# ScalarE takes 1-f and attention's output copies; x's sums keep their place; product orders change

## The chip, the cores and the metric

The program runs on one core of one Trainium2 chip. A time is device microseconds (us) of one execution. The kernel before has a median of 1113.62 us over three runs (1113.46 to 1114.1). Engines are named as the profile does: PE is TensorE, DVE is VectorE, ACT is ScalarE, POOL is GpSimd; SP starts DMAs. The profile is of one execution, and its lines are lines of the kernel before.

## The reference, cut to what matters

One layer over 256 tokens of width 2048, all in float32. The input is normed and projected to nine parts. Five of them belong to sixteen heads of a gated linear recurrence (q, v, forward gates, backward gates, output gate z_a), four to a short convolution, which the change leaves alone.

```python
hn = _rmsnorm(h, norm_w[i])
proj = hn @ w_in[i]
q, v, f_fwd, f_bwd, z_a, b_gate, c_gate, h_b, z_b = jnp.split(proj, IN_SPLITS, axis=-1)
# per direction:
f = lb + (1.0 - lb) * jax.nn.sigmoid(f_logit)
log_f = jnp.log(f)
k = 1.0 - f
# chunks of 64 tokens: q and k times exp of running sums of log_f, scores, masked, times v,
# plus what a carried state adds; forward and backward are summed
o_a = _head_rmsnorm(o_a, hgrn_norm_w[i]) * jax.nn.silu(z_a)
...
h = h + jnp.concatenate([o_a, o_b], axis=-1) @ w_out[i]
gate = jax.nn.sigmoid(h @ w_ple_gate[i])
h = h + (p[i] @ w_ple[i]) * gate
return _rmsnorm(h, final_norm_w)
```

So `k = 1 - f` is an affine map of the sigmoid, with two numbers per channel.

## The kernel before, in words

**Weights.** SP's queue loads tiles of w_in (128 x 2048 f32, `raw`, three buffers). The class `Stream` splits each half tile into a high and a low part, which together carry the value: ScalarE casts the high part (L121) and VectorE subtracts it to get the low one (L122). A split tile (`spl`, five buffers) is asked for three ahead of the products that read it. Splits are most of the work of both engines.

**Products.** A gate block (`gemm_in`) projects 256 channels: 16 k-tiles, each with four products on PE, two 128x512 ones (L428: high weights against both parts of x) and two 128x256 ones (L426: low weights against x's high part). A table `kicks` gives single k-tiles another order of these four: PLAIN is long, short, long, short; OUTER is long, short, short, long; SHORTS is both shorts and then both longs. `evac` sums the two halves of an accumulator (ScalarE copies one, L488, VectorE adds the other, L489).

**Stages.** Two heads are a pair. `two_pairs(i)` runs for i = 0, 2, 4, 6: for the pairs i and i+1 the blocks FF, FB (both gates) and Q, then `gemm_vz`, which makes v and z_a of four heads at once. For i = 2, 4, 6 three of its eight pairs of k-tiles are multiplied with seven products of sums in place of eight; for that, sums of x (`xsum`, from `xd`; `act_sums` L533 and L536, `act_split` L543 and L544) are made once, in the stage of i = 0, or whenever the scheduler lets them in.

**Attention's elementwise work.** `mix_forgets` of a pair: GpSimd multiplies by the tokens' norms (L493), ScalarE takes sigmoids (L615, L617), and for each direction and head the logarithm `lf` (L624, an ACTIVATE with a scale and a bias per channel); VectorE turns the sigmoid into 1-f in place (L628, the same kind of map, 128x256, four per pair). `mix_pair`: VectorE's scans of `lf` (L679, L685), differences (L692 to L703), ScalarE's exponentials (L704 to L707), VectorE's products with k and q (L708, L709), GpSimd's `kc`, `qc`, `kx` (L717, L723). PE's scores (L736) and `cx` (L780), then masks and copies. `outputs`: PE's four outputs `o` in PSUM (L798, L799), ScalarE's sums of squares of `o` (L803), VectorE's copy of `o` to `ogz` in SBUF (L804, 128x512, one per pair).

**The end of two pairs.** A stage later `finish_two` takes the square root of the mean squares (L643, ScalarE, 128x8), its reciprocal (L644) and scales `ogz` with it and with the output gate `zt` (eight 128x128 pieces, L649, VectorE). `turn` transposes each pair's `ogz` on PE (L659, four per pair) and splits it into `mixa` (L662, L663), from which the output projection reads.

**What sets the order.** A tile scheduler places each engine's instructions by priority; `tc.high_priority(offset=...)` lifts splits and sums of accumulators ahead of other work, and `tc.keep_in_program_order` pins an instruction to its written place. Attention's pieces are started at due times: `at(n, f)` calls f after n further ticks, and each k-tile of products ticks once. Within an engine the queue is then fixed; an instruction waits for its inputs, and all behind it wait too. Each time when ScalarE changes between functions of different tables, the program has an ACT_TABLE_LOAD.

Of the kernel before, what the change touches and what calls it, by code (L numbers as in the profile page):

```python
# [17 lines left out]
P = 128  # L18
# [119 lines left out]
def tile_hymba_encoder(  # L138
# [118 lines left out]
    cvw, th = vec[:, 3:6, :], vec[:, 6:10, :].rearrange("p (d j) c -> p d j c", d=2)  # L257


    wz = const.tile([P, P], F32, name="wz")  # L260
    dve.memset(wz, 0.0)

    act.activation(dummy[:, 0:1], wz[:, 0:1], AF.Copy)
# [8 lines left out]
    ones = const.tile([P, 1], F32, name="ones")  # L272
    pool.memset(ones, 1.0)

    early = const.tile([P, 2048], F32, name="early")
    smask = early[:, 0:T]
    pool.memset(smask, 1.0)
    pool.memset(smask.rearrange("p (c t) -> p c t", t=CH)[:, :, 0:1], 0.0)
# [16 lines left out]
        dve.memset(t, 0.0)  # L295


    mx = const.tile([P, 2, 16], F32, name="mx")
    et = const.tile([P, 2, 2, 16], F32, name="et")
    esum = const.tile([P, 2, 16], F32, name="esum")  # L300
# [72 lines left out]
    rbc = const.tile([P, T], F32, name="rbc")  # L373
    rbc2 = early[:, T : 2 * T]
    ss8 = const.tile([P, 2, 4], F32, name="ss8")
    rw = [const.tile([P, P], F32, name=f"rw{m}") for m in range(2)]

    def load_tokens(m):
        nc.sync.dma_start(xf32[:, 8 * m : 8 * m + 8].rearrange("p k t -> p (k t)"), xtok[:, m])
# [12 lines left out]
    def x_norms():  # L392
        dve.tensor_reduce(out=rx, in_=ss8, op=ALU.add, axis=AX.X)
        act.activation(rx, rx, AF.Sqrt, bias=epst, scale=1.0 / D)
        dve.reciprocal(out=rx, in_=rx)
        for m in range(2):
            dve.tensor_copy(rw[m], rx[:, m : m + 1].broadcast_to([P, P]))

    def norms_spread():
        rps = psm.tile([P, 512], F32, tag="y", name="rps")  # L400
        for m in range(2):
            pe.matmul(rps[:, m * P : (m + 1) * P], lhsT=rw[m], rhs=ident, start=True, stop=True)
        dve.tensor_copy(rbc, rps[:, :T])  # L403
        dve.tensor_tensor(out=rbc2, in0=rbc, in1=rbc, op=ALU.mult)

# [121 lines left out]
    at(14, norms_spread)  # L527


    def act_sums(src, a, s):  # L530


        dve.tensor_tensor(out=a, in0=src[:, :, 0], in1=src[:, :, 1], op=ALU.add)  # L533
        a11, a21, a12, a22 = (a[:, k, m * P : (m + 1) * P] for k in range(2) for m in range(2))
        for o, x, y in ((0, a21, a22), (1, a21, a11), (2, a11, s[:, 0]), (3, a12, s[:, 2])):
            dve.tensor_tensor(out=s[:, o], in0=x, in1=y, op=ALU.subtract)  # L536
# [74 lines left out]
    def mix_forgets(i, xf, qt):  # L611

        by_norms(xf.rearrange("p a b t -> p (a b) t"), rbc, 4)
        by_norms(qt, rbc, 2)
        act.activation(xf, xf, AF.Sigmoid)  # L615
        sg = ap_.tile([P, 2, T], F32, tag="sg", name=f"sq{i}")
        act.activation(sg, qt, AF.Sigmoid)  # L617
        pool.tensor_tensor(out=qt, in0=qt, in1=sg, op=ALU.mult)

        lf = ap_.tile([P, 2, 2, T], F32, tag="lf", name=f"lf{i}")  # L620
        for d in range(2):
            for h in range(2):
                hd = 2 * i + h
                act.activation(  # L624
                    lf[:, d, h, :], xf[:, d, h, :], AF.Ln,
                    bias=lb[:, d, hd : hd + 1], scale=oml[:, d, hd : hd + 1],
                )
                dve.tensor_scalar(  # L628
                    xf[:, d, h, :], xf[:, d, h, :], noml[:, d, hd : hd + 1], oml[:, d, hd : hd + 1],
                    op0=ALU.mult, op1=ALU.add,  # L630
                )
        return lf

# [34 lines left out]
    def mix_pair(i, xf, qt, lf, here=False):  # L668
# [121 lines left out]
        def outputs(vt, ogz, ss):  # L790

            s, sx = st
            o = psm.tile([P, 2, 2, P], F32, tag="y", name=f"o{i}")
            for h in range(2):
                c = (2 * (i % 2) + h) * P
                hs = slice(c, c + P)
                for m in range(2):
                    pe.matmul(o[:, m, h, :], lhsT=s[:, h, m, :], rhs=vt[:, m, hs], start=True, stop=False)  # L798
                    pe.matmul(o[:, m, h, :], lhsT=sx[:, h, 1 - m, :], rhs=vt[:, 1 - m, hs], start=False, stop=True)  # L799
            junk = ap_.tile([P, P], F32, tag="jk", name=f"jk{i}")  # L800
            for h in range(2):
                for m in range(2):
                    act.activation(junk, o[:, m, h, :], AF.Square, accum_out=ss[:, m, h : h + 1])  # L803
            dve.tensor_copy(ogz, o)  # L804

        return scores, outputs

# [5 lines left out]
    def two_pairs(i):  # L813
# [455 lines left out]
```

## Time and profile before

| | |
|---|---|
| median of 3 runs | 1113.62 us (1113.46 to 1114.1) |
| the profiled execution | 1113.2 us |
| its span in the trace | 1111.2 us |
| granted TensorE clock, mean | 0.998 |
| PE busy | 1100.2 us (99%), 6455 matmuls |
| VectorE busy | 854.4 us (77%) |
| ScalarE busy | 675.4 us (61%) |
| GpSimd busy | 267.1 us (24%) |
| L628, 1-f on VectorE | 32 x 442 ns = 13.9 us (with overlap) |
| L804, output copies on VectorE | 8 x 680 ns = 5.4 us |

Times in a timeline are microseconds from the span's start. The stages of two pairs begin, by PE's first product of each, at 7, 128, 240 and 357 us; the convolution's blocks begin at 475 us. An instruction's row in a timeline has its start, its duration, engine and line, and in brackets what ended the idle time ahead of it. A mean duration is longer than the time from start to start where an engine overlaps two instructions.

### The profile page before, as it was taken

The page shows a single profiled execution, that of the slowest core. Times are in us where ns is not written, and L with a number is a line of the kernel's source. Part 1 is how long each engine was busy: PE and PEld are TensorE (multiplying, and loading weights), DVE is VectorE, ACT ScalarE, POOL GpSimd, SP SyncE. Part 2 cuts the span into 40 slices and gives each one's busy share as a digit, 9 for nine tenths or more (in the row PEclk, how much of TensorE's full clock was granted, in tenths as well). Part 3 has the DMA queues.
Part 4 walks back from the last instruction along what each step waited for, and adds up shares of the span by engine and source line. Part 5 has one row for each costly group of instructions (what it writes and reads, how often), then busy time and mean ns, then how long its engine had stood idle before and what let it go on. Part 6 is the DMA issues. An engine that isn't in the chain of part 4 may idle for free.

```text
span 1111.2 us, 16886 instructions
## 1 busy us (share of the span) xinstructions
PE 1100.2 (99%) x6455; PEld 947.7 (85%) x6455; DVE 854.4 (77%) x1127; ACT 675.4 (61%) x946; POOL 267.1 (24%) x215
## 2 busy tenths in 40 slices
PE   9999999999999999999999999999999999999997
PEld 8888888888888888888888888888888888888886
DVE  7899468996889778998657848856767888877673
ACT  7787567767876697675535534534546575575562
POOL 1035116103430325043333223424331000000101
PEclk9999999999999999999999999999999999999999
DMA  9755555474447844658999998999979987887542
GB/s 349 271 166 172 183 190 169 135 265 152 159 147 263 305 152 152 224 171 234 299 305 262 255 340 222 289 328 264 290 202 297 326 297 286 288 312 251 196 133 76
DMA packets 69808, 260.44 MB, mean 234 GB/s; under 512 B 7008, under 2 KB 16608, under 8 KB 52192
## 3 DMA queue, kind: packets, MB, share of 16 engines
q1 hardware_dynamic: 60480, 242.25, 62.1%
q0 software_dynamic: 8960, 16.78, 9.8%
q8 instruction: 51, 0.84, 0.3%
q10 hardware_dynamic: 288, 0.34, 0.1%
q14 instruction: 29, 0.24, 0.1%
HBM read 257.25 MB, written 35.65 MB: 264 GB/s over the span
## 4 chain that ended last, share of the span: by engine, by line
PE 93%; DVE 3%; POOL 1%; issue 1%; ACT 1%; DMA 0%; DVEq 0%; ACTq 0%
PE a L428 36%; PE a L426 18%; PE avz L548 3%; PE avz L549 3%; PE avz L550 3%; PE pg L1030 3%; PE pg L1031 3%; PE pg L1029 3%; PE pa L548 2%; PE pa L550 2%; PE pa L549 2%; DVE spl L122 1%; PE pb_sc L550 1%; PE pb_sc L548 1%; PE pb_sc L549 1%; PE cx L780 1%
## 5 line engine op out<-in xcount | busy, mean ns | idle before, releaser
L122 DVE TENSOR_TENSOR spl<-raw,spl 128x1024 fp32r<-128x1024 f32 (+2 forms) x419 | 505.1, 1222 | 165.4 <-ACT spl L121 158.2
L428 PE MATMUL a<-xs,spl 128*128 128x512 f32 x1792 | 621.9, 393 | 0.6 <-DVE xs L368 0.6
L121 ACT CAST spl<-raw 128x1024 fp32r<-128x1024 f32 (+2 forms) x419 | 413.0, 999 | 250.3 <-PE a L426 96.4
L426 PE MATMUL a<-xs,spl 128*128 128x256 f32 x1792 | 494.8, 279 | 0.0
L428 PEld LDWEIGHTS a<-xs,spl 128*128 128x128 f32 x1792 | 334.0, 187 | 74.0 <-ACT spl L121 0.7
L426 PEld LDWEIGHTS a<-xs,spl 128*128 128x128 f32 x1792 | 337.1, 189 | 2.9 <-DVE spl L122 0.3
L1146 POOL TENSOR_TENSOR hh<-hh,fw 128x512 f32<-128x512 f32 (+1 forms) x9 | 10.9, 1225 | 250.7 <-ACT gt L1145 248.0
L488 ACT COPY r<-a 128x256 f32<-128x256 f32 x112 | 40.4, 368 | 34.6 <-PE a L426 33.0
L548 PE MATMUL avz<-spl,xs 128*128 128x512 f32 x138 | 54.0, 391 | 0.0
L550 PE MATMUL avz<-spl,xs 128*128 128x512 f32 x138 | 53.7, 389 | 0.0
L549 PE MATMUL avz<-spl,xs 128*128 128x512 f32 x138 | 53.7, 389 | 0.0
L717 POOL TENSOR_TENSOR qc<-pf,ge 128x256 f32<-128x256 f32 x16 | 22.0, 1379 | 106.7 <-ACT dd L707 89.1
L1029 PE MATMUL pg<-spl,ht 128*128 128x512 f32 (+1 forms) x120 | 45.2, 377 | 0.0
L1030 PE MATMUL pg<-spl,ht 128*128 128x512 f32 (+1 forms) x120 | 45.0, 375 | 0.0
L1031 PE MATMUL pg<-spl,ht 128*128 128x512 f32 (+1 forms) x120 | 45.0, 375 | 0.0
L493 POOL TENSOR_TENSOR xf<-xf,rbc 128x1024 f32<-128x1024 f32 x8 | 20.8, 2603 | 96.9 <-DVE rbc L403 49.5
L121 ACT CAST spl<-early 128x1024 fp32r<-128x1024 f32 (+1 forms) x29 | 28.7, 990 | 19.6 <-PE pb_y L550 7.5
L122 DVE TENSOR_TENSOR spl<-early,spl 128x1024 fp32r<-128x1024 f32 (+1 forms) x29 | 32.8, 1147 | 8.3 <-ACT spl L121 7.8
L548 PE MATMUL pa<-spl,mixa 128*128 128x512 f32 x88 | 34.5, 392 | 0.0
L550 PE MATMUL pa<-spl,mixa 128*128 128x512 f32 x88 | 34.3, 390 | 0.0
L549 PE MATMUL pa<-spl,mixa 128*128 128x512 f32 x88 | 34.3, 389 | 0.0
L946 POOL TENSOR_TENSOR cg<-cg,hb 128x512 f32<-128x512 f32 x8 | 13.7, 1718 | 79.2 <-DVE hb L489 79.2
(321 smaller groups left out, 1650.5 us busy)
## 6 DMA issues: line engine op xcount, KB each, us to landing
raw<-in_w_in_dram SPq DMA_DIRECT2D x106, 1024.0 KB, 7.0
raw<-in_w_in_dram SPq DMA_DIRECT2D x100, 256.0 KB, 3.9
raw<-in_w_out_dram SPq DMA_DIRECT2D x36, 512.0 KB, 5.6
sums<-in_w_out_dram SPq DMA_DIRECT2D x32, 512.0 KB, 10.4
raw<-in_w_in_dram SPq DMA_DIRECT2D x26, 512.0 KB, 5.5
raw<-sums SPq DMA_DIRECT2D x13, 1024.0 KB, 5.2
raw<-in_w_gate_dram SPq DMA_DIRECT2D x9, 1024.0 KB, 4.9
sums<-in_w_out_dram POOLq DMA_DIRECT2D x16, 512.0 KB, 10.5
```

The source lines that it names most:

```text
L121: self.nc.scalar.copy(out=v[:, :, 0], in_=r)
L122: self.nc.vector.tensor_tensor(out=v[:, :, 1], in0=r, in1=v[:, :, 0], op=ALU.subtract)
L426: pe.matmul(a[:, :T], lhsT=lhsT, rhs=xs[:, kt, 0, :], start=False, stop=(kt == NKT - 1))
L428: pe.matmul(a, lhsT=lhsT, rhs=xs[:, kt, :, :].rearrange("p s n -> p (s n)"), start=(kt == 0), stop=False)
L488: act.copy(out=r, in_=acc[m][:, 1, :])
L548: pe.matmul(acc, lhsT=ah, rhs=w[:, 0], start=start, stop=False)
L549: pe.matmul(acc, lhsT=ah, rhs=w[:, 1], start=False, stop=False)
L550: pe.matmul(acc, lhsT=al, rhs=w[:, 0], start=False, stop=stop)
L717: pool.tensor_tensor(out=c64(dst[:, d]), in0=c64(src[:, d, :, half * P : (half + 1) * P]), in1=g.unsqueeze(3).broadcast_to([P, 2, 2, CH]), ...
L1029: pe.matmul(acc[m], lhsT=lh, rhs=wh, start=(kt == 0), stop=False)
L1030: pe.matmul(acc[m], lhsT=lh, rhs=wl, start=False, stop=False)
L1031: pe.matmul(acc[m], lhsT=ll, rhs=wh, start=False, stop=(kt == nk - 1))
```

## The change

1. In `mix_forgets` 1-f moves from VectorE (`tensor_scalar`) to ScalarE (`activation` with Identity, the same scale and bias per channel): 32 instructions.
2. In `outputs` the copy of `o` moves from VectorE to ScalarE: 8 instructions.
3. The first instruction of each of x's sums keeps its place in program order.
4. Three k-tiles of pair 1's FB block (1, 5 and 9) go from one SHORTS (at 1) to three; the Q blocks of pairs 5 and 7 become plain (before: OUTER at 1, SHORTS at 5).
5. A few small tiles move to other buffers: `wz` into `early`, `mx`, `et` and `esum` into the pool `xp`, both `rw` into one tile with the tag of the scores.

```diff
@@ -257,7 +257,8 @@
-    wz = const.tile([P, P], F32, name="wz")
+    early = const.tile([P, 2048], F32, name="early")
+    wz = early[:, 1024 : 1024 + P]
     dve.memset(wz, 0.0)
...
-    mx = const.tile([P, 2, 16], F32, name="mx")
+    mx = xp.tile([P, 2, 16], F32, name="mx")
...
-    rw = [const.tile([P, P], F32, name=f"rw{m}") for m in range(2)]
...
+        rw.append(ap_.tile([P, 2, P], F32, tag="s", name="rw"))
...
-    def act_sums(src, a, s):
+    def act_sums(src, a, s, place=lambda instr: instr):
...
-        dve.tensor_tensor(out=a, in0=src[:, :, 0], in1=src[:, :, 1], op=ALU.add)
+        place(dve.tensor_tensor(out=a, in0=src[:, :, 0], in1=src[:, :, 1], op=ALU.add))
...
-                dve.tensor_scalar(
-                    xf[:, d, h, :], xf[:, d, h, :], noml[:, d, hd : hd + 1], oml[:, d, hd : hd + 1],
-                    op0=ALU.mult, op1=ALU.add,
+                act.activation(
+                    xf[:, d, h, :], xf[:, d, h, :], AF.Identity,
+                    bias=oml[:, d, hd : hd + 1], scale=noml[:, d, hd : hd + 1],
                 )
...
-            dve.tensor_copy(ogz, o)
+            act.copy(out=ogz, in_=o)
...
-                act_sums(xs[:, k : k + 2], a, t)
+                act_sums(xs[:, k : k + 2], a, t, tc.keep_in_program_order)
...
-            kicks = {(0, 1): ({}, ONE, BOTH), (2, 0): (ONE, BOTH, {}), (2, 1): ({}, {}, {})}
-            kicks |= {(4, 0): (ONE, TURNED, BOTH), (6, 0): (ONE, TURNED, BOTH)}
+            kicks = {(0, 1): ({}, {k: SHORTS for k in (1, 5, 9)}, BOTH), (2, 0): (ONE, BOTH, {}), (2, 1): ({}, {}, {})}
+            kicks |= {(i, e): ((ONE, TURNED, BOTH), ({}, {}, {}))[e] for i in (4, 6) for e in range(2)}
             kick = kicks.get((i, e), ({}, {}, BOTH if i + e else {}))
```

The scheduler moves more than the diff says. In the order of a program `spl` is a weight split, `ss` the squares' sums and their root, `ogz` the attention outputs, `pf`, `dd` and `ge` the exponentials' tiles, `sq` and `sz` the sigmoids of q and z_a, `r` the copy of an accumulator half, `x<-y` means that x is written from y; in the changed kernel lines from L400 on are numbered two higher.

ScalarE in the stage of i = 4, from pair 4's first exponentials on, the kernel before:

```order
L706 ACT_TABLE_LOAD
L706 ACTIVATE pf_2755<-dd_2756 128x512
L643 ACT_TABLE_LOAD
L643 ACTIVATE ss_1332<-ss_1332,epst 128x8
L121 CAST spl_2830<-raw_2809 128x4x256
L617 ACT_TABLE_LOAD
L617 ACTIVATE sq_2737<-qt_2354 128x512
L121 CAST spl_2851<-raw_2849 128x4x256
L638 ACTIVATE sz_0_2749<-zt_1331 128x512
```

The square root of pairs 2 and 3 stands behind the first exponential, ahead of the sigmoids. ScalarE with the change, where the square root stands now:

```order
L490 COPY r<-a_5_0_2786 128x256
L490 COPY r<-a_5_1_2787 128x256
L121 CAST spl_2926<-raw_2895 128x4x256
L709 ACT_TABLE_LOAD
L709 ACTIVATE dd_2754<-dd_2754 128x512
L121 CAST spl_2947<-raw_2945 128x4x256
L645 ACT_TABLE_LOAD
L645 ACTIVATE ss_1330<-ss_1330,epst 128x8
L121 CAST spl_2992<-raw_2945 128x4x256
```

It stands behind the sigmoids, behind the last of pair 4's exponentials and behind six more splits. The order for i = 6 changes in the same way.

VectorE in the same stage before, from the reciprocal of that root on:

```order
L644 RECIPROCAL ss_1332<-ss_1332 128x8
L122 TENSOR_TENSOR spl_2830<-raw_2809,spl_2830 128x4x256
L709 TENSOR_TENSOR pf_2755<-qt_2354,pf_2755 128x512
L122 TENSOR_TENSOR spl_2851<-raw_2849,spl_2851 128x4x256
L649 SCALAR_TENSOR_TENSOR ogz_2447<-ogz_2447,ss_1332,zt_1331 128x128 x2
L649 SCALAR_TENSOR_TENSOR ogz_2704<-ogz_2704,ss_1332,zt_1331 128x128 x2
L122 TENSOR_TENSOR spl_2878<-raw_2849,spl_2878 128x4x256
L649 SCALAR_TENSOR_TENSOR ogz_2447<-ogz_2447,ss_1332,zt_1331 128x128 x2
```

The scalings are spread among splits. VectorE with the change:

```order
L710 TENSOR_TENSOR dd_2754<-xf_2351,dd_2754 128x512
L122 TENSOR_TENSOR spl_2947<-raw_2945,spl_2947 128x4x256
L646 RECIPROCAL ss_1330<-ss_1330 128x8
L651 SCALAR_TENSOR_TENSOR ogz_2445<-ogz_2445,ss_1330,zt_1329 128x128 x4
L122 TENSOR_TENSOR spl_2992<-raw_2945,spl_2992 128x4x256
L651 SCALAR_TENSOR_TENSOR ogz_2702<-ogz_2702,ss_1330,zt_1329 128x128 x2
L491 TENSOR_TENSOR xf_2784<-a_5_0_2874,r 128x256
L651 SCALAR_TENSOR_TENSOR ogz_2702<-ogz_2702,ss_1330,zt_1329 128x128 x2
```

The reciprocal follows the root to its new place, and the scalings of the first pair stand together ahead of the second pair's. PE's transposes of `ogz` stand where they did.

x's sums on VectorE: before, two of the three start in the first pair's stage, behind the tokens' squares.

```order
L393 TENSOR_REDUCE few<-ss_176 128x2
L533 TENSOR_TENSOR xd<-xs 128x512
L536 TENSOR_TENSOR xd<-xd 128x128 x4
L533 TENSOR_TENSOR xd<-xs 128x512
L395 RECIPROCAL few<-few 128x2
L397 COPY rw_177<-few 128x128
```

With the change they stand in the stage of i = 2, between its splits.

```order
L122 TENSOR_TENSOR spl_1375<-raw_1354,spl_1375 128x4x256
L535 TENSOR_TENSOR xd<-xs 128x512
L538 TENSOR_TENSOR xd<-xd 128x128 x4
L122 TENSOR_TENSOR spl_1403<-raw_1401,spl_1403 128x4x256
L546 TENSOR_TENSOR xsum<-xd,xsum 128x4x128
```

More of the change, by code (lines that the diff above doesn't have):

```diff
@@ L273, in tile_hymba_encoder @@
     pool.memset(ones, 1.0)
-    early = const.tile([P, 2048], F32, name="early")
     smask = early[:, 0:T]
@@ L295, in tile_hymba_encoder @@
         dve.memset(t, 0.0)
-    mx = const.tile([P, 2, 16], F32, name="mx")
-    et = const.tile([P, 2, 2, 16], F32, name="et")
-    esum = const.tile([P, 2, 16], F32, name="esum")
+    mx = xp.tile([P, 2, 16], F32, name="mx")
+    et = xp.tile([P, 2, 2, 16], F32, name="et")
+    esum = xp.tile([P, 2, 16], F32, name="esum")
     lb = const.tile([P, 2, 16], F32, name="lb")
@@ L395, in x_norms @@
         dve.reciprocal(out=rx, in_=rx)
+        rw.append(ap_.tile([P, 2, P], F32, tag="s", name="rw"))
         for m in range(2):
-            dve.tensor_copy(rw[m], rx[:, m : m + 1].broadcast_to([P, P]))
+            dve.tensor_copy(rw[0][:, m], rx[:, m : m + 1].broadcast_to([P, P]))
+    rw = []
     def norms_spread():
@@ L401, in norms_spread @@
         for m in range(2):
-            pe.matmul(rps[:, m * P : (m + 1) * P], lhsT=rw[m], rhs=ident, start=True, stop=True)
+            pe.matmul(rps[:, m * P : (m + 1) * P], lhsT=rw[0][:, m], rhs=ident, start=True, stop=True)
         dve.tensor_copy(rbc, rps[:, :T])
```

## The prediction

> **What bounds the kernel now.** I read the page's head and its chain of waits first, then the timelines of the engines by stage. The head and the chain:
>
> ```profile
> span 1111.2 us, 16886 instructions
> PE 1100.2 (99%) x6455; PEld 947.7 (85%) x6455; DVE 854.4 (77%) x1127; ACT 675.4 (61%) x946; POOL 267.1 (24%) x215
> PE 93%; DVE 3%; POOL 1%; issue 1%; ACT 1%; DMA 0%; DVEq 0%; ACTq 0%
> ```
>
> TensorE is busy for 99% of the span and is 93% of the chain. So a lighter VectorE is worth nothing by itself: the change can only win where PE waits or paces slowly, and loses wherever it makes PE wait. Between its first product and the tail I find one real wait of PE. It stands in the first pair's stage, here in PE's timeline with the two engines behind it (start, duration, engine, line; idle before in brackets):
>
> ```profile
> 113.12 1.16 PE L780 MATMUL cx<-qc,kx 128*128 128x128 f32 x8 [1.06 <-POOL kx L723]
> ...
> 111.16 1.91 POOL L723 TENSOR_TENSOR kx<-kc,ge 128x512 f32<-128x512 f32 x1
> ...
> 99.98 0.63 ACT L706 ACTIVATE pf<-dd 128x512 f32<-128x512 f32 x1 [5.11 <-DVE gx L701]
> ```
>
> PE waits 1.06 us for GpSimd's kx, which hangs on the exponentials, for which ScalarE had idled 5.11 us behind VectorE.
>
> **1-f and the copies, unit prices.** In the groups by line (count, busy us, mean ns, idle before):
>
> ```profile
> L628 DVE TENSOR_SCALAR xf<-xf,noml,oml 128x256 f32<-128x256 f32 x32 | 13.9, 442 | 4.6 <-ACT lf L624 4.6
> L624 ACT ACTIVATE lf<-xf,lb,oml 128x256 f32<-128x256 f32 x32 | 18.3, 597 | 0.1
> L804 DVE COPY ogz<-o 128x512 f32<-128x512 f32 x8 | 5.4, 680 | 1.1 <-ACT jk L803 1.1
> L787 ACT COPY sx<-cx 128x512 f32<-128x512 f32 x8 | 4.6, 579 | 5.1 <-PE cx L780 5.1
> ```
>
> VectorE loses 13.9 + 5.4 us. The trace has no Identity; its nearest row is L624, of the same shape with the same two per-partition operands: 597 ns, and 0.50 us from start to start (two of them fill 274.24 to 275.23 below). A copy takes 0.50 us likewise (579 ns, overlapped). In total ScalarE gains 32 x 0.50 + 8 x 0.50 = 20 us, and at 61% busy it has room. What matters is where.
>
> **The turn of pairs 4 and 5 (and 6 and 7), the main term.** In the middle of a block PE turns the previous pairs' outputs, eight transposes of ogz, and then goes on with that block's products:
>
> ```profile
> 301.04 1.03 PE L659 MATMUL ogt<-ident,ogz 128*128 128x128 f32 x8
> 301.83 0.48 PE L428 MATMUL a<-xs,spl 128*128 128x512 f32 x1
> ...
> 418.54 1.03 PE L659 MATMUL ogt<-ident,ogz 128*128 128x128 f32 x8
> ```
>
> They stand at the same places of PE's order before and after; the first four read one ogz, the last four the other, from 301.04 + 4 x 0.11 = 301.47. Each ogz is first scaled on VectorE (L649), which needs the reciprocal (L644) of ScalarE's square root (L643). In ScalarE's timeline before:
>
> ```profile
> 269.48 1.06 ACT L615 ACTIVATE xf<-xf 128x1024 f32<-128x1024 f32 x1 [1.46 <-POOL xf L493]
> ...
> 274.24 1.09 ACT L624 ACTIVATE lf<-xf,lb,oml 128x256 f32<-128x256 f32 x2
> 275.23 1.03 ACT L121 CAST spl<-raw 128x1024 fp32r<-128x1024 f32 x1
> ...
> 277.65 0.28 ACT L803 ACTIVATE jk<-o 128x128 f32<-128x128 f32 x1 [0.88 <-PE o L799]
> ...
> 283.95 0.30 ACT L643 ACTIVATE ss<-ss,epst 128x8 f32<-128x8 f32 x1
> ...
> 288.55 0.63 ACT L638 ACTIVATE sz<-zt 128x512 f32<-128x512 f32 x1 [0.47 <-POOL qt L618]
> ...
> 299.87 1.03 ACT L121 CAST spl<-raw 128x1024 fp32r<-128x1024 f32 x1
> ```
>
> The square root ran at 283.95, 17 us ahead of the transposes. The order of the changed kernel puts it right ahead of the split that began at 299.87, behind both gates' sigmoids and the last exponential. From the sigmoid at 269.48 to that split the two orders hold the same ScalarE work, seven table loads each, but for four Identities and one output copy more. The sigmoid's start cannot move: it waits for GpSimd, which waits for PE's scores. So the split starts at 299.87 + 4 x 0.50 + 0.50 = 302.4, less the waits of ScalarE in that stretch (0.88 + 0.47 + 0.1 about an exponential), which a fuller queue swallows: its squares come at 278.2, after PE's output at 277.65. That is 300.9, and the square root ends at about 301.0. I see no new wait in the stretch: the chunk decays' inputs are ready by 279.9, ScalarE comes to them at 280.8.
>
> Behind it VectorE still has to work, by these rows:
>
> ```profile
> 284.76 0.19 DVE L644 RECIPROCAL ss<-ss 128x8 f32<-128x8 f32 x1
> ...
> 291.57 1.48 DVE L649 SCALAR_TENSOR_TENSOR ogz<-ogz,ss,zt 128x128 f32<-128x128 f32 x4 [1.20 <-POOL zt L639]
> 292.98 1.21 DVE L122 TENSOR_TENSOR spl<-raw,spl 128x1024 fp32r<-128x1024 f32 x1
> ...
> 297.07 0.75 DVE L489 TENSOR_TENSOR xf<-a,r 128x256 f32<-128x256 f32 x2
> 297.74 0.60 DVE L649 SCALAR_TENSOR_TENSOR ogz<-ogz,ss,zt 128x128 f32<-128x128 f32 x2
> ```
>
> In its new order: reciprocal 0.2, four scalings 1.4 (292.98 - 291.57), a split 1.1, two scalings 0.5, one sum of accumulators 0.3, two scalings 0.6: 4.1 us, with 0.1 for handing over. The second ogz is ready at 305.25, PE wants it at 301.47: **a wait of 3.8 us**, with everything on PE queued behind it, and nothing later that would give it back, since PE is the bound to the end. The stage of pairs 6 and 7 is a copy of this one 117.5 us later (418.54 against 301.04) with the same new order: 3.8 us again. **Sum +7.6 us.** Bounds: an Identity as cheap as the narrower copies L488 (two in 0.5 us, so 0.25) gives 2.8 a turn; ScalarE's waits all remaining gives 5.3. With Identities and copy free it would be 1.3. I take 3.8, since L624 is the same form.
>
> **The first pair.** VectorE's groups from 54 to 95.3 us, where it had nearly no idle time:
>
> ```profile
> L628 DVE TENSOR_SCALAR xf<-xf,noml,oml 128x256 f32<-128x256 f32 x8 | 4.3, 543 | 0.0
> L536 DVE TENSOR_TENSOR xd<-xd 128x128 f32<-128x128 f32 x8 | 3.0, 409 | 0.1
> L544 DVE TENSOR_TENSOR xsum<-xd,xsum 128x512 fp32r<-128x512 f32 x3 | 2.0, 681 | 0.0
> L533 DVE TENSOR_TENSOR xd<-xs 128x512 f32<-128x512 f32 x1 | 0.7, 692 | 0.0
> ```
>
> 10.0 us leave this stretch: 1-f to ScalarE, x's sums to the next stage (128 to 157 us), where VectorE waits at every split and both find room. ScalarE gets eight Identities (4.0 us), loses three casts of the sums (0.6 each) and its 5.11 us wait. The last logarithm stays near 90 us, VectorE is ready for the scans at about 91.5 instead of 95.4, so exponentials and kx come about 4 us earlier; 1.06 is all PE can gain. **-1.06 us** (0 if ScalarE slips by 3 us there).
>
> **Pairs 2 and 3.** Here PE runs close to its suppliers (VectorE's rows, then PE's):
>
> ```profile
> 200.01 0.42 DVE L489 TENSOR_TENSOR qt<-a,r 128x256 f32<-128x256 f32 x1
> ...
> 207.06 0.85 DVE L122 TENSOR_TENSOR spl<-raw,spl 128x512 fp32r<-128x512 f32 x1
> ...
> 203.79 0.62 ACT L121 CAST spl<-raw 128x512 fp32r<-128x512 f32 x1
> ...
> 211.01 0.39 PE L548 MATMUL ey<-spl,xsum 128*128 128x512 f32 x1
> ```
>
> Up to the 512-wide split ScalarE gets four Identities and one table load more (1.30 us from start to start), while a copy of 0.5 moves behind: 203.79 + 2.0 + 1.3 - 0.5 = 206.6, end 207.2, so VectorE starts its part 0.14 late, and the piece that PE reads at 211.01, done 0.1 us before, comes just in time. I take **0**, bounds 0 and +1.
>
> The Trainium skill, page "ScalarE: Activation LUTs", section "What ACT_TABLE_LOAD costs", counts 2.66 us for a switch, load and drain; by it this piece would be 1.4 us late and the sum 1.4 higher. The trace's 1.30 is used.
>
> **Product orders.** PE's timeline, fifteen k-tiles in the plain block and in the next one with two changed k-tiles:
>
> ```profile
> 289.94 0.39 PE L428 MATMUL a<-xs,spl 128*128 128x512 f32 x1
> ...
> 300.34 0.39 PE L428 MATMUL a<-xs,spl 128*128 128x512 f32 x1
> ...
> 302.61 0.39 PE L428 MATMUL a<-xs,spl 128*128 128x512 f32 x1
> ...
> 313.18 0.40 PE L548 MATMUL avz<-spl,xs 128*128 128x512 f32 x1
> ```
>
> 10.40 us plain, 10.57 with the changed order, which throws PE into the slower of its two steady paces (the first stages run in it too). Two such blocks turn plain: **-0.34 us**, or 0 if PE comes out of the wait in the slow pace. The block that gets three changed k-tiles runs in the slow pace; a changed k-tile there did not end it, so 0, at best -0.3 for that block and the next. The tiles that move into other buffers touch nothing but the first microseconds, where GpSimd's fill now follows the 13 warming products and GpSimd is idle until 53 us: 0.
>
> **Sum:** 7.6 - 1.06 - 0.34 = +6.2. The profiled execution took 1113.2 us (span 1111.2, 2.0 around it), the median of the runs is 1113.62: **1119.8 us**, a span of about 1117.4.
>
> **Rivals.** (1) *Half the price*: the added ScalarE work costs next to nothing in that stretch, so the turns wait 1.3 us each: 1113.62 + 2.6 - 1.4 = 1114.8. For it: ScalarE idles 39% of the time. Against it: from 269 to 301 it idles 1.5 us in all. (2) *Not slower*: ScalarE's queue runs ahead far enough that the square root still clears the transposes. Place: the split at 299.87; it decides if the square root ends before 297.2, 3.8 us ahead of my sum; then only the gains are left, 1112.2. For it: VectorE feeds the exponentials sooner. Against it: ScalarE waits for VectorE nowhere in that stretch, and L624 never takes under 586 ns. (3) *PE also loses its pace*: the products that warm PE in the first microseconds are shown below; they run at half the pace of the same form later (0.21 us against 0.11 in the transposes' row), for 3.7 us or more.
>
> ```profile
> L266 PE MATMUL wps<-wz 128*128 128x128 f32 x26 | 4.8, 369 | 1.1 <-DVE wz L261 1.1
> ```
>
> If the wait threw PE back into that state for as long, it would cost about 1.9 us a turn: 1119.8 + 3.8 = 1123.6. The four first transposes split the wait into 1.2 and 2.6 us, which speaks against it. The Trainium skill, page "TensorE: Matmul & The Clock Gate", section "What's actually happening", has half rate follow an idle window of about 3.4 us; by it a wait in two pieces would not trigger it.
>
> **How the numbers follow.** Forecast 0.72, own range 1117.8 to 1122.8 (turns 2.8 to 5.3 each); half price 0.11; not slower 0.09; lost pace 0.08. The range 1114.5 to 1122.5 takes in half the price and leaves out the not-slower case, the lost pace and the forecast's edges. A change under 0.2% (2.2 us) can't be told from none: slower has the forecast, the lost pace and a little of half the price, 0.82; same has most of half the price and of the not-slower case, 0.16; faster 0.02.
>
> **What would show it.** PE idle ahead of the L659 transposes near 301 and 418, released by VectorE's scaling of ogz, near 3.8 us each; no idle ahead of cx near 113; still seven table loads of ScalarE from the sigmoid to the square root; the two blocks behind the turns at 10.40 us per fifteen k-tiles. If PE does not wait at the turns, the main term is wrong; if it waits elsewhere, at 200 or 211, the zero for pairs 2 and 3 is.

## The result, and the profile after

The changed kernel takes 1125.88 us (median of four runs, 1124.1 to 1127.46) against 1113.54 us of the kernel before measured beside it: 1.011 times as long, 95% interval 1.0095 to 1.0125. The forecast was 1119.8 us, between 1114.5 and 1122.5. The direction was right; the size forecast, 6.2 us, was half of the 12.3 us that came, and the time lies outside the range.

The head of the page and of the chain, the changed kernel (this execution is the longest of its four, 1127.46 us):

```profile
span 1125.7 us, 16884 instructions
PE 1112.8 (99%) x6455; PEld 951.7 (85%) x6455; DVE 829.2 (74%) x1087; ACT 702.0 (62%) x990; POOL 258.5 (23%) x215
PE 90%; ACT 5%; DVE 1%; POOL 1%; issue 1%; DMA 1%; DVEq 0%; SPq 0%; ACTq 0%
```

VectorE is 25 us lighter, ScalarE 27 us heavier, and PE is busy for 12.6 us longer with the same 6455 products. So most of the loss does not look like idle time at all: PE takes longer over the same work. ScalarE now has 5% of the chain, where it had 1%.

Since the products are the same ones, and stand in the same order but for the swapped ones and three transposes at each of two turns, the start of the n-th product in one trace less that in the other tells how late PE is by then. Differences of that lag between a few places, after less before, in us:

| stretch of PE's order | forecast | trace after |
|---|---|---|
| start, first stage up to cx | 0 | -0.3 |
| the wait ahead of cx (113 us) | -1.06 | -1.13 |
| from cx to the turn of pairs 4 and 5's stage | 0 | +0.7 |
| that turn, 25 products from the last one ahead of it | +3.8 | +3.9 |
| between the turns | -0.17 | +0.5 |
| the turn one stage later | +3.8 | +4.1 |
| from there to just behind the last outputs (518 us of before) | -0.17 | +0.2 |
| the convolution (518 to 854 us of before) | 0 | +6.1 |
| output projection to the end | 0 | +0.6 |
| sum | +6.2 | +14.6 |

The cx wait came out as sized, and so did the turns, these by two errors that cancel (below). The stretch from 198 to 240 us, where the forecast had put 0 for pairs 2 and 3, is 0.0. The convolution, which the forecast put at nothing, took 6.1 us. The sum is above 12.3 us since this execution is the longest of its four.

**Ahead of cx.** PE's timeline after; there is no idle time in brackets any more:

```profile
111.69 1.16 PE L782 MATMUL cx<-qc,kx 128*128 128x128 f32 x8
```

**The turn.** ScalarE's, then VectorE's timeline of the changed kernel ahead of the first turn:

```profile
295.32 1.28 ACT L709 ACT_TABLE_LOAD   x1
296.61 0.63 ACT L709 ACTIVATE dd<-dd 128x512 f32<-128x512 f32 x1
297.15 1.03 ACT L121 CAST spl<-raw 128x1024 fp32r<-128x1024 f32 x1
298.20 1.28 ACT L645 ACT_TABLE_LOAD   x1
299.50 0.30 ACT L645 ACTIVATE ss<-ss,epst 128x8 f32<-128x8 f32 x1
```

```profile
299.83 0.20 DVE L646 RECIPROCAL ss<-ss 128x8 f32<-128x8 f32 x1
300.14 1.45 DVE L651 SCALAR_TENSOR_TENSOR ogz<-ogz,ss,zt 128x128 f32<-128x128 f32 x4
301.51 1.21 DVE L122 TENSOR_TENSOR spl<-raw,spl 128x1024 fp32r<-128x1024 f32 x1
302.65 0.60 DVE L651 SCALAR_TENSOR_TENSOR ogz<-ogz,ss,zt 128x128 f32<-128x128 f32 x2
303.17 0.41 DVE L491 TENSOR_TENSOR xf<-a,r 128x256 f32<-128x256 f32 x1
303.51 0.60 DVE L651 SCALAR_TENSOR_TENSOR ogz<-ogz,ss,zt 128x128 f32<-128x128 f32 x2
```

The square root ends at 299.80. The sigmoid that opens the stretch starts 1.19 us earlier than before here (268.29 against 269.48), so in the old time that is 300.99: the forecast's 301.0. VectorE's chain behind it takes 4.3 us, forecast 4.1 with 0.1 for handing over. PE's timeline:

```profile
300.17 0.28 PE L428 MATMUL a<-xs,spl 128*128 128x256 f32 x1
300.86 0.33 PE L661 MATMUL ogt<-ident,ogz 128*128 128x128 f32 x1 [0.41 <-DVE ogz L651]
301.38 0.59 PE L661 MATMUL ogt<-ident,ogz 128*128 128x128 f32 x3 [0.20 <-DVE ogz L651]
303.04 0.48 PE L661 MATMUL ogt<-ident,ogz 128*128 128x128 f32 x1 [1.07 <-DVE ogz L651]
303.17 0.78 PE L430 MATMUL a<-xs,spl 128*128 128x512 f32 x1
303.74 0.41 PE L428 MATMUL a<-xs,spl 128*128 128x256 f32 x1
303.96 0.63 PE L430 MATMUL a<-xs,spl 128*128 128x512 f32 x1
304.38 0.84 PE L661 MATMUL ogt<-ident,ogz 128*128 128x128 f32 x3
...
306.46 0.39 PE L430 MATMUL a<-xs,spl 128*128 128x512 f32 x1
```

The fifth transpose starts at 303.04, when the first scaled piece of the second ogz is there (302.99), not when the whole tile is (304.11): a transpose waits for its own piece. It was said ahead of the prediction that PE's transposes stand where they did. At this turn and the next that holds for five of the eight: in the changed program's order for PE the last three come behind three of the block's products (303.17 to 303.96 here), and by then their pieces are ready. So the wait is 2.3 us (0.6 + 0.4 + 1.3 over the usual time from start to start), not 3.8. But then the products run at half their pace up to 306.3: a 512-wide one 0.63 us, where 0.39 is usual. The table by windows of the changed kernel has the granted clock behind POOL's column:

```profile
302.00:304.00 2.00, 0.96 (x4) 0.87 (x4) 2.00 (x6) 0.60 (x2) 0.00 (x0) 0.74 0.05 12
304.00:306.00 2.00, 2.00 (x9) 1.72 (x9) 2.00 (x5) 0.48 (x1) 0.34 (x1) 0.50 0.89 276
306.00:308.00 2.00, 2.00 (x12) 1.72 (x11) 1.24 (x3) 0.86 (x2) 2.00 (x1) 0.91 0.70 240
```

By the trace's clock record it is 0.50 from 302.95 to 306.37, 3.41 us, and costs about 1.6 us more. Two errors cancelled: the wait was oversized by 1.5, the half clock was left to a rival.

**The convolution.** One row by windows for the same 120 us, the kernel before, and then the changed one (PE busy and its products come first):

```profile
540.00:660.00 120.00, 120.00 (x694) 105.80 (x693) 81.10 (x108) 55.20 (x76) 37.64 (x32) 1.00 0.95 294
```

```profile
540.00:660.00 120.00, 120.00 (x681) 104.03 (x680) 79.19 (x108) 55.84 (x76) 35.89 (x30) 1.00 0.95 281
```

PE is busy for all of it in both, at the full granted clock in both, and does 681 products instead of 694: 1.9% fewer. This is the slower of the two steady paces, 707 ns a k-tile against 693. It begins neither at a turn nor with the convolution's first blocks, but behind the outputs of the last pair, 7, some 40 us into them. PE's timeline before, from the last output on:

```profile
512.23 0.39 PE L799 MATMUL o<-vt,sx 128*128 128x128 f32 x2
512.37 0.48 PE L428 MATMUL a<-xs,spl 128*128 128x512 f32 x1
512.68 0.28 PE L426 MATMUL a<-xs,spl 128*128 128x256 f32 x1
512.80 0.40 PE L428 MATMUL a<-xs,spl 128*128 128x512 f32 x1
513.04 0.28 PE L426 MATMUL a<-xs,spl 128*128 128x256 f32 x1
513.15 0.39 PE L428 MATMUL a<-xs,spl 128*128 128x512 f32 x1
```

and after:

```profile
520.03 0.39 PE L801 MATMUL o<-vt,sx 128*128 128x128 f32 x2
520.17 0.48 PE L430 MATMUL a<-xs,spl 128*128 128x512 f32 x1
520.49 0.28 PE L428 MATMUL a<-xs,spl 128*128 128x256 f32 x1
520.61 0.39 PE L430 MATMUL a<-xs,spl 128*128 128x512 f32 x1
520.84 0.28 PE L428 MATMUL a<-xs,spl 128*128 128x256 f32 x1
520.96 0.40 PE L430 MATMUL a<-xs,spl 128*128 128x512 f32 x1
```

Nothing waits, and the rows agree within 0.02 us; but from the fifth product on the starts stand 230 and 117 ns apart before, 231 to 241 and 113 to 120 ns after. The same happens in the changed kernel behind the outputs of pairs 3 and 5 (277 and 395 us in the time of before), and once behind transposes, those of pairs 0 and 1 (184 us); there the kernel before stays fast. In these places the next v and z_a products or the next turn bring PE back; behind the last outputs nothing does, and the slow pace lasts to the end of the convolution. The first fall is 117 us ahead of the first turn at which PE waits: these waits are not its cause.

### The profile page after: what moved, and what is told of

The parts are those of the page before. It is cut to its first block, busy times and chain, and to the rows that moved or that the text cites. A ratio compares the mean times of both kernels' runs of the same rounds, so it can differ in the third digit from the quotient of the medians.

```text
span 1125.7 us, 16884 instructions
## 1 busy us (share of the span) xinstructions
PE 1112.8 (99%) x6455; PEld 951.7 (85%) x6455; DVE 829.2 (74%) x1087; ACT 702.0 (62%) x990; POOL 258.5 (23%) x215
## 4 chain that ended last, share of the span: by engine, by line
PE 90%; ACT 5%; DVE 1%; POOL 1%; issue 1%; DMA 1%; DVEq 0%; SPq 0%; ACTq 0%
PE a L430 33%; PE a L428 17%; PE avz L550 3%; PE avz L552 3%; PE avz L551 3%; PE pg L1032 3%; PE pg L1033 3%; PE pg L1031 3%; ACT spl L121 1%; PE pa L551 1%; PE pa L552 1%; PE pa L550 1%; PE a L449 1%; PE a L451 1%; PE a L450 1%; PE pb_sc L551 1%
## 5 line engine op out<-in xcount | busy, mean ns | idle before, releaser
L430 PE MATMUL a<-xs,spl 128*128 128x512 f32 x1792 | 631.4, 399 | 0.0
```

What stands on the lines that cost most here:

```text
L430: pe.matmul(a, lhsT=lhsT, rhs=xs[:, kt, :, :].rearrange("p s n -> p (s n)"), start=(kt == 0), stop=False)
```

## Experiments

In each run's trace the lag behind the kernel before is taken over the same stretches; turn 1 and turn 2 are those near 301 and 418 us. That is one profiled execution; the ratios are of several timed ones.

| run | median us | ratio (95%) | cx | turn 1 | turn 2 | convolution |
|---|---|---|---|---|---|---|
| changed kernel | 1125.88 | 1.0110 (1.0095 to 1.0125) | -1.13 | 3.91 | 4.11 | 6.08 |
| 1 product orders undone | 1125.59 | 1.0113 (1.0093 to 1.0133) | -1.13 | 2.61 | 4.01 | 6.09 |
| 2 output copies undone | 1120.16 | 1.0055 (1.0040 to 1.0070) | -1.13 | 0.46 | 0.50 | 6.09 |
| 3 1-f undone | 1124.90 | 1.0099 (1.0084 to 1.0114) | -1.13 | 2.36 | 2.36 | 6.09 |
| 4 square root ahead | 1118.55 | 1.0044 (1.0027 to 1.0061) | -1.13 | -0.02 | -0.02 | 6.09 |
| 5 small tiles undone | 1120.62 | 1.0069 (1.0043 to 1.0095) | -1.13 | 3.04 | 3.05 | -0.01 |
| 6 before + small tiles | 1120.32 | 1.0054 (1.0035 to 1.0072) | 0.00 | -0.01 | -0.01 | 6.08 |
| 7 both 4 and 5 | 1112.70 | 0.9988 (0.9976 to 1.0000) | -1.13 | 0.03 | 0.03 | 2.85 |
| 8 as 4, an order changed in the convolution | 1117.79 | 1.0029 (1.0018 to 1.0040) | -1.13 | -0.02 | -0.02 | 5.04 |
| 9 before + scores moved | 1120.03 | 1.0056 (1.0042 to 1.0071) | 0.00 | -0.01 | -0.01 | 5.06 |
| 10 before + weights 2 KB lower | 1114.67 | 1.0007 (0.9994 to 1.0020) | -1.13 | 0.01 | 0.02 | 3.09 |
| 11 before + weights 1 KB lower | 1114.07 | 1.0004 (0.9993 to 1.0014) | 0.00 | 0.01 | 0.02 | -0.01 |
| 12 before + x's sums in place | 1113.62 | 0.9997 (0.9985 to 1.0009) | -1.13 | 0.01 | 0.02 | 3.04 |
| 13 before + kx moved | 1113.38 | 0.9998 (0.9984 to 1.0011) | 0.00 | 0.01 | 0.02 | 0.01 |
| 14 changed, square root ahead, scores back | 1112.83 | 0.9991 (0.9980 to 1.0002) | -1.13 | 0.03 | 0.03 | 2.30 |

(The run before beside them had medians of 1113.54 to 1114.03.)

### Four parts undone, one at a time: runs 1 to 4

Run 1, the product orders of before in the changed kernel:

```diff
-            kicks = {(0, 1): ({}, {k: SHORTS for k in (1, 5, 9)}, BOTH), (2, 0): (ONE, BOTH, {}), (2, 1): ({}, {}, {})}
-            kicks |= {(i, e): ((ONE, TURNED, BOTH), ({}, {}, {}))[e] for i in (4, 6) for e in range(2)}
+            kicks = {(0, 1): ({}, ONE, BOTH), (2, 0): (ONE, BOTH, {}), (2, 1): ({}, {}, {})}
+            kicks |= {(4, 0): (ONE, TURNED, BOTH), (6, 0): (ONE, TURNED, BOTH)}
```

> The changed kernel with the product orders of before (one SHORTS in pair 1's FB block, OUTER and SHORTS in the Q blocks of pairs 5 and 7); all else as changed. Theory 'orders': PE's slow steady pace in the convolution (14 blocks of two gate blocks, 22.61 against 22.19 us) comes from the changed orders, so it is gone: 1125.9 - 6 = 1119.9, turns still +4.1 each. Theory 'ScalarE work' (the copy or 1-f on ScalarE leaves PE in the slow pace behind the outputs) and theory 'addresses' (the moved tiles): the pace stays slow, 1125.9, at most 0.5 off for the Q blocks.

1125.59 us, and the convolution is as slow as in the changed kernel. The orders are not its cause, and their change is worth nothing that the times can tell.

Run 2, the output copies back on VectorE:

```diff
-            act.copy(out=ogz, in_=o)
+            dve.tensor_copy(ogz, o)
```

> The changed kernel with the output copies (ogz from o) back on VectorE. The square root then stands one split earlier in ScalarE's queue, so each turn should wait 1 to 1.5 us less: -2 to -3 by every theory. Theory 'copy' (ScalarE's copy of o out of PSUM right behind the outputs leaves PE in its slow pace): also -6, 1117. Theories 'orders', '1-f', 'addresses': the convolution stays slow, 1123 to 1124.

1120.16 us: 5.7 less, by the traces all of it at the turns (7.1 there), the convolution slow. ScalarE's, then PE's timeline of this run:

```profile
295.34 1.28 ACT L645 ACT_TABLE_LOAD   x1
296.63 0.30 ACT L645 ACTIVATE ss<-ss,epst 128x8 f32<-128x8 f32 x1
```

```profile
300.27 0.73 PE L661 MATMUL ogt<-ident,ogz 128*128 128x128 f32 x5
301.19 0.59 PE L661 MATMUL ogt<-ident,ogz 128*128 128x128 f32 x3 [0.19 <-DVE ogz L651]
```

The square root is 2.87 us earlier than in the changed kernel, by one split, one table load and the copy; that clears nearly all of the wait, and the clock stays whole. I had expected 2 to 3 us in sum.

Run 3, 1-f back on VectorE:

```diff
-                act.activation(
-                    xf[:, d, h, :], xf[:, d, h, :], AF.Identity,
-                    bias=oml[:, d, hd : hd + 1], scale=noml[:, d, hd : hd + 1],
+                dve.tensor_scalar(
+                    xf[:, d, h, :], xf[:, d, h, :], noml[:, d, hd : hd + 1], oml[:, d, hd : hd + 1],
+                    op0=ALU.mult, op1=ALU.add,
                 )
```

> The changed kernel with 1-f back on VectorE. ScalarE has four Identities (2.0 us) and a split (1.0) less ahead of the square root: the turns' waits of 2.4 us are gone, and with them the half clock behind them (1.7 us each): -8 by every theory. The wait ahead of cx at 113 us should return in part (+0 to +1.3). Theory '1-f' (ScalarE's added load leaves PE in the slow pace): also -6, 1112. Others: 1118.

1124.90 us, a miss by every theory: 2 us less of Identities and a split less bring the square root forward by 1.5 us only (it starts at 298.01), among others because ScalarE now idles 0.89 us ahead of its squares, and VectorE has one split more between its scalings. PE's timeline, and the windows of this run:

```profile
300.42 0.49 PE L661 MATMUL ogt<-ident,ogz 128*128 128x128 f32 x3
301.29 0.33 PE L661 MATMUL ogt<-ident,ogz 128*128 128x128 f32 x1 [0.38 <-DVE ogz L651]
302.69 0.33 PE L661 MATMUL ogt<-ident,ogz 128*128 128x128 f32 x1 [1.07 <-DVE ogz L651]
303.54 0.59 PE L661 MATMUL ogt<-ident,ogz 128*128 128x128 f32 x3 [0.17 <-DVE ogz L651]
```

```profile
304.00:306.00 2.00, 2.00 (x13) 1.72 (x13) 2.00 (x4) 0.83 (x2) 0.70 (x1) 1.00 0.85 252
```

About the same idle time as in the changed kernel, but the clock stays at 1.00: 2.4 us a turn instead of 3.9 to 4.1. So the half clock is what stands between. With the rest of the change in place, undoing either move alone, 1-f's or the copies', leaves the square root behind the last exponentials. The wait ahead of cx is gone here too: 1-f on ScalarE is not what removes it.

Run 4, the square root ahead by priority, all else as changed:

```diff
-        act.activation(ss, ss, AF.Sqrt, bias=epst, scale=1.0 / P)
-        dve.reciprocal(out=ss, in_=ss)
+        with tc.high_priority(offset=200):
+            act.activation(ss, ss, AF.Sqrt, bias=epst, scale=1.0 / P)
+            dve.reciprocal(out=ss, in_=ss)
```

> The changed kernel with the square root of finish_two and its reciprocal put ahead by priority, so that they stand six splits earlier, where before had them. No wait and no half clock at the turns: -8.2. If the slow pace of the convolution has nothing to do with those waits: 1117.7. If the waits (and the half clock behind them) leave PE in the slow pace: 1111.5.

1118.55 us: 7.3 less. ScalarE's, then PE's timeline:

```profile
282.71 1.28 ACT L646 ACT_TABLE_LOAD   x1
284.00 0.30 ACT L646 ACTIVATE ss<-ss,epst 128x8 f32<-128x8 f32 x1
```

```profile
300.37 1.03 PE L662 MATMUL ogt<-ident,ogz 128*128 128x128 f32 x8
```

The square root is back at 284.00 and the transposes run without a wait, with all the added work still on ScalarE (and five table loads from the sigmoid to the split at the turn, in place of seven). This shows the main term: not the load, but the square root's place in the queue. The convolution stays slow without any wait at the turns, so the two losses are separate.

### What leaves PE in the slow pace: runs 5, 6, 9 to 11 and 13

What runs 1 to 4 have in common with the changed kernel are the small tiles and the place of x's sums; the latter run 12 has alone, and it leaves the last outputs in the fast pace. Run 5 undoes them in the changed kernel, run 6 makes that change alone in the kernel before (the first lines of the change's diff, backwards and forwards).

> The changed kernel with its small tiles where before had them (wz, early, mx, et, esum, rw), so that x's parts, the weight tiles and the splits lie 2 KB higher in each partition again. Four runs left PE in the slow pace behind the first pair's outputs whichever of the other parts was undone. Theory 'addresses': where the tiles lie decides in which pace PE comes out of the outputs; the convolution is fast again, 1125.9 - 6.4 = 1119.5, with the turns as in the changed kernel. Theory 'any change upstream' (the pace is a matter of the moment in which PE comes to the products, and any shift of it changes the pace): stays slow, 1125.9.

> The kernel before with the moved tiles alone. Theory 'addresses': slow pace behind the outputs of every stage and through the convolution, 1113.6 + 6.4 = 1120. Theory 'any change upstream': PE's work and its moments are those of before but for the first microseconds, so the pace stays fast: 1113.6.

Run 5 has the convolution of before (-0.01) with the turns' waits, though its four times spread from 1118.45 to 1126.09 us; run 6 has the slow convolution (+6.08) and nothing else of the change in it. Run 6's row by windows:

```profile
540.00:660.00 120.00, 120.00 (x681) 104.08 (x681) 79.37 (x109) 55.27 (x76) 35.56 (x30) 1.00 0.96 285
```

So 6 us of the loss come from where tiles lie. By the addresses in the two programs the change does two things: x's parts, weight tiles and splits lie 2 KB lower in each partition, and, since rw is the first tile with the scores' tag, attention's scores s get the place at the bottom of their pool (20 KB lower), and the tiles from lf to kx move up by 2 KB, kx into the scores' old place. Runs 9 and 10 part these.

Run 9, rw with the scores' tag, the room it leaves filled, so that x's parts, weights and splits stay:

```diff
-    rw = [const.tile([P, P], F32, name=f"rw{m}") for m in range(2)]
+    pad = const.tile([P, 256], F32, name="pad")
...
+        rw.append(ap_.tile([P, 2, P], F32, tag="s", name="rw"))
```

> The kernel before with rw as one tile with the scores' tag, and 1 KB of padding in its old place: x's parts, the weight tiles and the splits lie exactly as before, only the scores s lie 20 KB lower and the tiles from lf to kx 2 KB higher. Theory 'scores' (where the outputs' operands lie decides in which pace PE leaves the outputs): slow behind the outputs and through the convolution, 1120. Theory 'weights' (where x's parts and the splits lie, from which the products behind read): fast, 1113.8.

Run 10, all small tiles moved, but rw in the pool xp, so that the scores stay (run 11: rw where before had it, so the weights lie 1 KB lower):

```diff
-        rw.append(ap_.tile([P, 2, P], F32, tag="s", name="rw"))
+        rw.append(xp.tile([P, 2, P], F32, name="rw"))
```

> The kernel before with the small tiles moved, but rw in the pool with mx: x's parts, the weight tiles and the splits lie 2 KB lower, the scores and all of attention's tiles as before. Theory 'weights': slow, 1120. Theory 'scores': fast, 1113.8.

> As the run with the weights moved, by 1 KB instead of 2. Theory 'weights': if the pace hangs on how far the tiles lie from others, either can come, slow (1120) or fast (1113.8); theory 'scores': fast.

Run 13, rw with kx's tag: kx goes to the bottom, lf to qc move up, the scores stay.

```diff
-        rw.append(ap_.tile([P, 2, P], F32, tag="s", name="rw"))
+        rw.append(ap_.tile([P, 2, P], F32, tag="kx", name="rw"))
```

> As the run with the scores moved, but rw has kx's tag: kx lies 18 KB lower, lf to qc 2 KB higher, and the scores s where before had them. If the scores' own place sets the pace behind the outputs: fast there, 1114.0. If the shift of the other attention tiles does it: slow, 1120.

Runs 9 and 13 differ in one word, and hold the same instructions in the same order on every engine; only s and kx lie elsewhere. By windows, run 9 and then run 13:

```profile
540.00:660.00 120.00, 120.00 (x681) 104.06 (x680) 77.80 (x107) 56.51 (x75) 39.94 (x32) 1.00 0.96 286
```

```profile
540.00:660.00 120.00, 120.00 (x694) 105.81 (x693) 79.51 (x108) 55.53 (x75) 36.05 (x31) 1.00 0.96 293
```

1120.03 against 1113.38 us. Moving weights and x's parts by 1 or 2 KB (runs 10, 11) leaves the pace behind the outputs as it was. It is the place of the scores: in all eight traces with the scores at the bottom of the pool (the changed kernel, runs 1 to 4, 6, 8 and 9) PE leaves the last outputs in the slow pace, and in all eight with the old place (before, 5, 7 and 10 to 14) in the fast one; the same holds behind the outputs of pairs 3 and 5. The scores are among what PE reads in those outputs, right ahead of the products that part. The outputs do not read kx, but in all eight slow traces kx lies 2 KB higher as well, and no run moves it up alone, so that it has no part is argued and not shown. Why the scores' place matters was not found, and it is not all: behind the transposes of pairs 0 and 1, which do not read the scores, runs 6 and 9 stay fast, while the changed kernel and runs 1 to 4 and 8 do not.

### An order in the convolution, and versions without the losses: runs 8, 12, 7 and 14

Run 8, on top of run 4: two k-tiles of a convolution block in other orders.

```diff
-        evac(gemm_in(B_CG, i, {} if i else ONE), lambda m: cg[:, m, :], ctmp)
+        evac(gemm_in(B_CG, i, {1: BOTH}.get(i, {}) if i else ONE), lambda m: cg[:, m, :], ctmp)
```

> The changed kernel with the square root ahead, and in the first convolution block of i = 1 two k-tiles in other orders (OUTER at 1, SHORTS at 5). If an order can bring PE out of the slow pace for good, the 12 blocks behind it run fast: 1118.6 - 5.3 = 1113.3. If the pace comes back by itself (something present in the whole convolution sets it), the gain ends within a block: 1118.4.

1117.79 us, the pace unmoved by it; in this trace PE gets fast at 787.5 us, behind the one changed k-tile that both kernels have at the end of the convolution. In run 9 that k-tile does the same, in the changed kernel it does nothing. Orders do turn the pace, but not reliably.

Run 12, the kernel before with x's sums in program order, and nothing else (the `place` lines of the diff).

> The kernel before with the one part that I expect to gain: x's sums kept in program order. The run with 1-f undone had no wait ahead of cx, so 1-f on ScalarE is not needed for it: PE's wait of 1.06 us at 113 us is gone, nothing else moves, 1113.9 - 1.3 = 1112.6. If 1-f's move or the copies' are needed as well: 1113.9.

The cx wait is gone (PE's timeline of this run):

```profile
112.12 1.16 PE L780 MATMUL cx<-qc,kx 128*128 128x128 f32 x8
```

and 1-f and the copies are not needed for it. (In run 10 it is gone as well: by its trace PE comes there 1.6 us later, and kx is ready only 0.3 us later.) Yet the median is 1113.62 beside 1114.03, no difference that can be told. In this execution the gain is given back 560 us later:

```profile
673.48 0.39 PE L428 MATMUL a<-xs,spl 128*128 128x512 f32 x1
674.34 0.39 PE L426 MATMUL a<-xs,spl 128*128 128x256 f32 x1 [0.47 <-DVE spl L122]
```

A split comes 0.47 us late (VectorE makes sums for the output projection just ahead of it), and from there PE is in the slow pace, but for a few microseconds, up to 783 us: +3.04 in the convolution. The traces of runs 7, 10 and 14 lose the fast pace at 673 to 677 us too, in run 7 behind a wait of 0.18 us, in 10 and 14 without one; those of 5, 11 and 13 keep it. So the fast pace of this kernel is easily lost. That this is why single times lie between 1111 and 1118 us in runs 7 and 10 to 14 fits, but is not shown, since only one execution of each was traced.

Run 7 joins runs 4 and 5; run 14 joins run 4 with rw in xp, as in run 10.

> The changed kernel with the square root ahead and the old tiles: both losses away. Theory 'addresses': 1118.6 - 6.4 = 1112.2, 1.4 faster than before (the wait ahead of cx). Otherwise 1118.6.

> The changed kernel with the square root ahead and rw in the pool with mx, so that the scores lie where before had them; the other tiles stay as changed. If the late square root and the scores' place are all that the change lost: 1111.5 to 1112.7, 1.3 to 2 less than before. If the 2 KB shift of the weights costs anything by itself, or another loss is left: 1114 or more.

1112.70 and 1112.83 us, some 13 us under the changed kernel: the late square root and the scores' place are the whole loss, as far as the times can tell. Against the kernel before they are 0.9988 and 0.9991, intervals that end at 1.0000 and 1.0002; both medians lie 1.1 to 1.3 us below, about the cx wait, but neither is faster by more than can be told from no change.

## Where the prediction was right and where it failed

- **What bounds it, right.** PE's waits and pace decide; VectorE's 25 us saved gave nothing.
- **The main term, right in cause and by luck in size.** The square root's place, its end (300.99 in the old time, forecast 301.0) and VectorE's chain (4.3, forecast 4.2) came as worked out, and run 4 shows the cause. An Identity takes 0.50 us from start to start, as assumed (273.05 to 273.55). But of the idle time of ScalarE that the sum let a fuller queue swallow, the 0.47 us ahead of sz are still there, so the end was met partly by luck.
- **The wait itself, oversized.** I let PE wait for the whole second ogz (305.25), with all eight transposes together; the fifth needs only the first piece, and the last three stand later in the new order. 2.3 us, not 3.8. Of the 1.5 between, 0.4 is time that PE had already lost in the slow pace behind pair 3's outputs; in run 5, which keeps the fast pace there, the turns cost 3.05 us each at the full clock.
- **The half clock, left to a rival.** In place of the missing wait came the half clock, which I had put at 1.9 us a turn and 0.08: it appeared in the changed kernel's trace at both turns, at 1.5 to 1.8 us each. The reasoning against it, that the wait is split in two, was wrong: PE's idle times there are 0.41, 0.20 and 1.07 us, and the clock fell within 0.9 us of their end. Nor does such a wait always bring it: with 1.6 to 2.1 us of idle time runs 3 and 5 kept the full clock at both turns, and run 1 at its first one, where the idle times are 0.44, 0.20 and 1.06 us.
- **The Trainium skill's rule**, page "TensorE: Matmul & The Clock Gate", section "What's actually happening", that half rate follows an idle window of about 3.4 us, would have had no half clock here. The trace has it with 1.7 us of idle time in three pieces, and for 3.41 us, about the length of that window. The same section says that the window runs free, which fits the traces: the clock first rises at 3.96 us in one of them and at 6.95 us in another.
- **What the clock record adds.** In all 16 traces the granted clock, once it has risen, changes only at whole multiples of 3.413 us from there. Laid on this grid, the idle time of the three turns with half clock falls mostly into one step of it: 1.59, 1.61 and 1.72 us. At the five others a boundary splits it, and no step holds more than 1.42 us, even in run 5. As far as eight turns show, what differed was where the wait lay on the grid. This gives no threshold: in run 6 the first step behind the rise (6.7 to 10.1 us) holds 1.63 us, and the clock stayed whole.
- **The cx wait, right**: -1.06 forecast, -1.13 measured. Run 12 shows that x's sums do it alone.
- **The orders, wrong**: -0.34 forecast, no gain measured (run 1). I read from one trace that the old orders throw PE into the slow pace in the Q blocks. In the traces of runs 10 to 13, which have them, PE is fast behind them (from 306.6 us in run 11) and 0.13 us ahead of before's trace between the turns; in runs 7 and 14, plain, the Q block is slow and PE 0.15 to 0.25 behind. Over all 16 traces the Q block behind the first turn is slow in five of the eight with the plain order and in one of the eight with the old one: if anything the gain has the other sign, by some 0.3 us a stage, too little for the times to show.
- **The failed step**: "The tiles that move into other buffers touch nothing but the first microseconds ... 0." It measured +6.1 in the convolution, and +0.7 and +0.5 in front of the turns (with the tiles alone, run 6: 6.08, 0.46 and 0.31). I looked at what the move of rw, mx and wz does to instructions and waits, and found nothing, rightly: there is none. What moved was the scores' address. The prediction had the two paces in hand, with the numbers to price a fall (its 10.40 and 10.57 us per fifteen k-tiles are 11 ns a k-tile, 5 us over the convolution's 14 times 32 behind the last outputs; 14 ns and 6 us by the paces above), but asked only which orders would turn them. That rival should have stood there: PE leaves the last outputs in the slow pace, and nothing brings it back.
- **The range** reached 1122.5 and left out 1125.9 mainly for that reason: less the convolution's 6.1 us the time is 1119.8, inside it. Run 5, with the pace kept, has a median of 1120.6, though its turns kept the full clock as well.

## What to carry to other kernels

When work is moved onto an engine with room, look in its new order for what was pushed back, not at its load: here the added ScalarE work cost nothing that the times could tell once a square root of 0.3 us had its old place again. When PE is the bound and its trace shows more than one steady pace at the full granted clock, count each change that could move PE from one to the other as a term, at the difference times all the k-tiles up to the next place that resets it; a tile that only changes its buffer is such a change.

## What the runs showed of the hardware

- PE has two steady paces for the same products, 693 and 707 ns a k-tile, both with PE busy and the granted clock at 1.00, and keeps either for hundreds of microseconds. Which one it takes behind a block of 128-wide outputs hung on the place of one of these outputs' weights, the scores, in SBUF (runs 9 and 13, where kx differs too), 20 KB apart, and not on 1 or 2 KB for the tiles of the products themselves (runs 10 and 11). It fell behind waits of 0.2 to 0.5 us too (runs 7 and 12), but at the same place also without one (runs 10 and 14).
- Less than 2 us of idle time, in three pieces within 2.6 us, can halve PE's granted clock for 3.41 us, and need not: the clock fell at three turns and stayed whole at five with 1.6 to 2.1 us. It changed only on a grid of 3.413 us; where it fell, one step held 1.59 us or more of the idle time, at the five others at most 1.42; behind the first rise, in run 6, a step with 1.63 us did not halve it.
